# First modulation rounds packed by pairs of feature tiles, and five strips multiplied pair by pair

## The chip, the cores and the metric

The kernel runs on one core of a Trainium2 chip, in one launch. The metric is device time in microseconds (us). Before the change three runs gave 2202.88, 2203.56 and 2204.67 us; the median is 2203.56 us.

## The reference, cut to what matters

Two blocks of two layers each work on 256 tokens with 1024 features, in float32. The change touches only the start of layer 0 of the first block:

```python
mod = jax.nn.silu(c) @ w_ada + b_ada                 # (1, 1024) @ (1024, 3072)
shift, scale, gate = jnp.split(mod, 3, axis=-1)
h = _rmsnorm(x, norm_g) * (1.0 + scale[:, None, :]) + shift[:, None, :]
proj = h @ w_in                                      # (256, 1024) @ (1024, 6680)
(rq, rk, rv, rg, xbc, dt_raw, z, fq, fk, fv, fg, f_raw) = jnp.split(proj, IN_OFFSETS, axis=-1)
...
xbc = jax.nn.silu(_causal_dwconv(xbc, conv_w, conv_b))
dt = jax.nn.softplus(dt_raw + dt_bias)
```

Nothing can be multiplied by w_in before h is there, and a feature tile of h needs the norm of x and that tile's shift and scale, which are columns of w_ada.

## The kernel before, in words

Weights lie in device memory as one stream of *strips* in the order of their use (WPLAN, `wall`), each 128 partitions by up to 1024 columns, 512 KB. `_fetch` (L483) loads a strip into a tile `raw`, and splits it: ScalarE (ACT) copies it, rounded, to `hi` (L476), VectorE (DVE) subtracts that to get `lo` (L503). The tiles `hi` and `lo` have three buffers each; strip 3, one of EXTRA, uses tiles that are free at that time (`ret_o`, `fox_v`). `mm3` (L526) multiplies with three matmuls for each of the eight feature tiles of h (L530 to L532), each 128x256 here, so a strip takes 24. Strips 0 to 3 are B and C of the state-space branch, and each goes through `conv4`, a convolution of four taps in three DVE instructions on the PSUM bank (L472, tile `cv_y`). Strip 4 holds dt and the forget gates and goes into `dtf`, some 25 small DVE instructions. Strips 5 and on alternate between convolutions and parts of the attention branch. PSUM has three banks `mm`, three `aux` and two `tr`.

The modulation is made in *rounds* of 512 columns of w_ada: `ada_load` brings 2 MB in two transfers, `ada_round` (L683) multiplies them by silu(c) on TensorE (PE; L697, 32 records of the trace for each transfer), ACT copies the row, PE transposes it (L704), and DVE adds the bias into `mod`. Rounds 0 and 1 are the shift, rounds 2 and 3 the scale of feature tiles 0 to 3 and 4 to 7. They come in the order 0, 2, 1, 3 (FIRST_ROUNDS), so that `first_norm` can finish h (tiles `h_hi` on ACT, `h_lo` on DVE) for tiles 0 to 3 after two rounds and for tiles 4 to 7 after the other two. Before that x is normalised: squares on ACT, sums on DVE, a column sum on PE (L614), a reciprocal root in some ten small DVE instructions, a broadcast on PE (L623), and eight products into `qk_fox`. `spread` (L749) broadcasts silu(c) over the partitions for later rounds, which DVE does itself (L740). Here the names read `yd`, `qk_ret`, `xs`, `xdt` for the four tiles that hold the two transfers of a round, in turn, since these tiles are free at that time.

All transfers of weights are issued by SyncE (SP) in the order of the program. The order of the instructions on an engine is fixed when the program is built: it follows the order of the code, priorities (`prio`) and `issue_after`, which puts an instruction behind another. On the chip each engine takes its instructions in that order and waits for the one at the head.

Of the kernel before, what the change touches and what calls it, by code (L numbers as in the profile page):

```python
# [10 lines left out]
F32 = mybir.dt.float32  # L11
# [7 lines left out]
P = 128  # L19
# [149 lines left out]

FIRST_ROUNDS = (0, 2, 1, 3)


def _ada_plan():
    s = []
    for name, rounds in (("w_ada", 6), ("ada_w_2", 12)):
        for l in range(2):
            order = FIRST_ROUNDS + (4, 5) if (name, l) == ("w_ada", 0) else range(rounds)
            for r in order:  # L180
                for q in range(4):
                    if (1 if name == "w_ada" else 2, l, r) in ON_PE:
                        s.append((name, l, _full(2, 256 * q), ((512 * r, 512),)))
                    else:
                        s.append((name, l, None, ((512 * r + P * q, P),)))
    return s
# [178 lines left out]
class Kern:  # L365
# [117 lines left out]
    def _fetch(self):  # L483
        spec = WPLAN[self.wpos]
        w = _width(spec)
        nm = f"{self.wpos}"
        raw = self.wp.tile([P, 1024], F32, tag="raw", name="raw" + nm, bufs=RAW_BUFS)
        self.nc.sync.dma_start(out=raw[:, :w], in_=self.wall[self.woff:self.woff + P * w].rearrange("(p w) -> p w", p=P))
        if self.wpos in EXTRA and self.wpos < N_PLAN1:
            hi, lo = [self.bt([P, 1024], tag, FR, 1) for tag in ("ret_o", "fox_v")]  # L490
        elif self.wpos in EXTRA:
            hi, lo = [self.s4([P, 1024], FR, h + nm) for h in ("hi", "lo")]
        else:
            hi = self.wp.tile([P, 1024], FR, tag="hi", name="hi" + nm)
# [71 lines left out]
        while self.bg:  # L566
            self.bg.popleft()()

    def proj_f(self, name, act, T0, T, behind=None):

        w = self.strip(name)
        ps = self.mm_bank()
        with self.tc.issue_after(behind.ins) if behind else nullcontext():
            self.mm3(ps[:, :T], w, [(a[:, T0:T0 + T], b[:, T0:T0 + T]) for a, b in act])
        return ps[:, :T]

    def proj_t(self, name, act, tiles):
# [92 lines left out]
    def ada_load(self, which, l, r, tags=None):  # L670

        parts = []
        m = 2 if tags else 1
        for q in range(0, 4, m):
            spec = APLAN[self.apos]
            assert spec[0] == ("w_ada", "ada_w_2")[which - 1] and spec[1] == l and spec[3][0][0] == 512 * r
            t = self.bt([P, 2, 1024], tags[q // 2], F32, 1) if tags else self.s4([P, 1, 1024], F32, f"ada{which}{l}_{r}")
            n = m * P * 1024
            self.nc.sync.dma_start(out=t, in_=self.aall[self.aoff:self.aoff + n].rearrange("(m p w) -> p m w", p=P, m=m))
            self.aoff += n  # L680
            self.apos += m
            parts += [t[:, i] for i in range(m)]
        return parts  # L683

    def ada_round(self, which, l, r, parts):

        nc = self.nc
        nm = f"ada{which}{l}_{r}"
# [12 lines left out]
        s = self.ncpool.tile([P, P], F32, tag="ada_s", name=nm + "s", bufs=1)  # L701
        self.act(s, ps[:, :P], AF.Copy)
        pt = self.ps("tr")
        nc.tensor.transpose(pt[:, :P], s, self.ident)  # L704
        b = self.v(("b_ada%d" if which == 1 else "ada_b2%d") % l, 4 * r, 4)
        for i, m in enumerate(self.mods[which, l]):
            col = 0 if which == 1 else 1 + i
            self.add(m[:, 4 * r:4 * r + 4], pt[:, col:P:32], b)

    def new_mods(self, which, l):  # L710
        n = 24 if which == 1 else 48
# [34 lines left out]
        if q == 3:  # L746
            self.adaq.popleft()

    def spread(self, which, pool):  # L749

        self.cb[which] = [pool.tile([P, 1024], F32, tag=f"cb{which}{i}", name=f"cb{which}{i}", bufs=1) for i in range(which)]

        def piece(i, half):
            ps = self.ps("aux")
# [90 lines left out]
    def layer1(self, l):  # L845
# [6 lines left out]
        lo = self.bt([P, KD, 256], "h_lo", FR, 1)  # L852
        h = self.pairs(hi, lo, 8)
        if l == 0:
            self.first_norm(rb, h)
        else:
            mod = self.mods[1, l][0]
            self.modulate(self.b1, [([x[:, k] for k in range(KD)], 0, 256, self.v(f"norm_g{l}"), mod[:, 8:16], mod[:, 0:8], rb)], h)
            self.hold(HOLD)
        mod = self.mods[1, l][0]  # L860
        BC = self.bt([P, 4, 256], "BC", F32, 1)
        for n in range(4):

            behind = self.round_mm[(1, 0) + BEHIND[n]] if l == 0 and n < len(BEHIND) else None
            self.conv4(l, self.proj_f("w_in", h, 0, T, behind), 8 + n, BC[:, n])
            self.pump()
        ps = self.proj_f("w_in", h, 0, T)
        self.dtf(l, ps)
        cbm = self.bt([P, 2, 384], "cbm", F32, 1)
        for g in range(2):  # L870
# [108 lines left out]
    def first_norm(self, rb, h):  # L979
# [7 lines left out]
        for half in range(2):
            for r in FIRST_ROUNDS[2 * half:2 * half + 2]:
                self.adaq.popleft()
                if r != FIRST_ROUNDS[0]:  # L990
                    self.ada_round(1, 0, r, self.ada_load(1, 0, r, self.first_tags()))
                if r == FIRST_ROUNDS[SPREAD]:
                    for f in self.spread(1, self.b1):
                        f()
            if half == 0:
                for _ in range(3):
                    self._fetch()
            mod = self.mods[1, 0][0]
            c = slice(4 * half, 4 * half + 4)
            self.stt(a[:, c], mod[:, 8 + 4 * half:12 + 4 * half], 1.0, g[:, c], ALU.add, ALU.mult)  # L1000
            for k in range(4 * half, 4 * half + 4):
# [16 lines left out]
    def dtf(self, l, ps):  # L1018
        nc = self.nc
        sg, cr = self.c("sgn"), self.c("carry")  # L1020
        b = self.ncpool.tile([P, 4], F32, tag="dtf_b", name=f"dtf_b{l}")
        self.mul(b[:, 0:1], self.v(f"dtf_b{l}"), sg)

        self.act(b[:, 1:2], self.v(f"a_log{l}"), AF.Exp)
        self.ts(b[:, 1:2], b[:, 1:2], -1.0, ALU.mult)
# [825 lines left out]
    def run(self):  # L1851
# [102 lines left out]
```

## Time and profile before

| | us |
|---|---|
| median of three runs | 2203.56 |
| profiled execution, its own time | 2205.41 |
| its span, from the first to the last instruction | 2203.6 |
| PE busy | 2150.6 (98%) |
| DVE busy | 1714.0 (78%) |
| ACT busy | 1001.4 (45%) |

The profiled execution is one run, 1.85 us above the median. PE is busy nearly everywhere but at the start and in a few short stretches, so what matters is what PE waits for and when.

### The profile page before, as it was taken

What the parts mean: (1) busy time and instruction counts of PE and PEld (TensorE: products, weight loads), DVE (VectorE), ACT (ScalarE), POOL (GpSimd) and SP (SyncE); (2) the same over time, 40 slices, a digit from 0 to 9 for tenths busy, and PEclk for the clock granted to TensorE, in tenths of its full rate; (3) what the DMA queues carried; (4) which work ended last, traced back from release to release, by engine and by line L of the source; (5) the groups of instructions that cost most, each with busy time, mean ns of one, the idle gap of its engine ahead of it and who ended that gap; (6) DMA issues with size and microseconds to landing.
All of it is one profiled execution on the core that took longest, in us unless ns stands there. A gap on an engine that the chain in (4) does not pass through costs nothing. (4 is left out here: it accounts for less than half of the span.)

```text
span 2203.6 us, 38200 instructions
## 1 busy us (share of the span) xinstructions
PE 2150.6 (98%) x14481; PEld 1918.2 (87%) x14481; DVE 1714.0 (78%) x3551; ACT 1001.4 (45%) x1828; POOL 69.8 (3%) x654
## 2 busy tenths in 40 slices
PE   6999999999999999999999999999999999999999
PEld 5999989898877888888888888888888999999999
DVE  5986889888885899775575777666689977577977
ACT  4556455555445423432333443324355434445654
POOL 0000000000000000000000000000000000000000
PEclk9999999999999999999999999999999999999999
DMA  7665846467321134335353244453432353674665
GB/s 292 197 197 175 270 134 199 146 199 268 105 67 54 54 109 150 97 110 158 123 157 103 88 133 120 131 176 124 131 106 82 115 168 114 213 250 146 189 193 162
DMA packets 98088, 330.71 MB, mean 150 GB/s; under 512 B 10864, under 2 KB 14320, under 8 KB 97648
## 3 DMA queue, kind: packets, MB, share of 16 engines
q1 hardware_dynamic: 97456, 326.47, 46.5%
q8 instruction: 114, 1.87, 0.3%
q0 software_dynamic: 448, 1.81, 0.2%
q14 instruction: 70, 0.57, 0.1%
HBM read 325.08 MB, written 3.15 MB: 149 GB/s over the span
## 5 line engine op out<-in xcount | busy, mean ns | idle before, releaser
L476 ACT ACTIVATE hi<-raw 128x1024 fp32r<-128x1024 f32 (+3 forms) x494 | 492.0, 997 | 712.8 <-PE mm L531 445.0
L503 DVE TENSOR_TENSOR lo<-raw,hi 128x1024 fp32r<-128x1024 f32 (+3 forms) x494 | 564.8, 1144 | 234.9 <-ACT hi L476 231.2
L530 PE MATMUL mm<-h,hi 128*128 128x512 f32 (+1 forms) x1296 | 445.2, 344 | 3.3 <-ACT th L476 1.2
L532 PE MATMUL mm<-h,lo 128*128 128x512 f32 (+1 forms) x1296 | 441.9, 342 | 2.6 <-DVE lo L503 2.6
L531 PE MATMUL mm<-h,hi 128*128 128x512 f32 (+1 forms) x1296 | 441.9, 342 | 0.4 <-DVE h L472 0.4
L530 PEld LDWEIGHTS mm<-h,hi 128*128 128x128 f32 x1296 | 244.7, 189 | 32.8 <-ACT h L476 1.5
L532 PEld LDWEIGHTS mm<-h,lo 128*128 128x128 f32 x1296 | 245.0, 189 | 31.9 <-DVE lo L503 3.4
L531 PEld LDWEIGHTS mm<-h,hi 128*128 128x128 f32 x1296 | 244.8, 189 | 30.0 <-DVE h L472 0.8
L530 PE MATMUL mm<-hi,h 128*128 128x256 f32 x608 | 173.4, 285 | 1.6 <-ACT h L476 1.6
L531 PE MATMUL mm<-lo,h 128*128 128x256 f32 x608 | 172.5, 284 | 1.2 <-DVE lo L503 1.2
L532 PE MATMUL mm<-hi,h 128*128 128x256 f32 x608 | 173.0, 285 | 0.1
L530 PE MATMUL mm<-h_hi,hi 128*128 128x256 f32 x512 | 145.4, 285 | 4.2 <-ACT h_hi L476 2.5
L532 PE MATMUL mm<-h_hi,lo 128*128 128x256 f32 x512 | 145.3, 285 | 1.1 <-DVE lo L503 1.0
L531 PE MATMUL mm<-h_lo,hi 128*128 128x256 f32 x512 | 145.6, 286 | 0.5 <-DVE h_lo L454 0.5
L472 DVE SCALAR_TENSOR_TENSOR cv<-glu,vec,cv 128x512 f32<-128x512 f32 (+1 forms) x240 | 136.3, 613 | 2.5 <-ACT cv L476 2.5
L740 DVE SCALAR_TENSOR_TENSOR ada<-ada,cb 128x1024 f32<-128x1024 f32 x104 | 126.7, 1219 | 1.4 <-DMA ada<-aall 0.9
L530 PEld LDWEIGHTS mm<-hi,h 128*128 128x128 f32 x608 | 115.6, 190 | 3.3 <-ACT h L476 2.4
L531 PEld LDWEIGHTS mm<-lo,h 128*128 128x128 f32 x608 | 115.5, 190 | 2.1 <-DVE lo L503 1.4
L532 PEld LDWEIGHTS mm<-hi,h 128*128 128x128 f32 x608 | 115.7, 190 | 1.0 <-DVE h L472 0.7
L530 PEld LDWEIGHTS mm<-h_hi,hi 128*128 128x128 f32 x512 | 97.8, 191 | 5.3 <-ACT h_hi L476 2.9
L532 PEld LDWEIGHTS mm<-h_hi,lo 128*128 128x128 f32 x512 | 97.9, 192 | 1.7 <-DVE lo L503 1.7
L531 PEld LDWEIGHTS mm<-h_lo,hi 128*128 128x128 f32 x512 | 97.9, 191 | 1.3 <-DVE h_lo L454 0.9
(675 smaller groups left out, 4826.4 us busy)
## 6 DMA issues: line engine op xcount, KB each, us to landing
raw<-wall SPq DMA_DIRECT2D x400, 512.0 KB, 3.7
ada<-aall SPq DMA_DIRECT2D x120, 512.0 KB, 4.1
raw<-wall SPq DMA_DIRECT2D x32, 384.0 KB, 3.1
raw<-wall SPq DMA_DIRECT2D x32, 320.0 KB, 3.0
raw<-wall SPq DMA_DIRECT2D x32, 256.0 KB, 2.6
yd<-aall SPq DMA_DIRECT2D x2, 1024.0 KB, 10.4
qk_ret<-aall SPq DMA_DIRECT2D x2, 1024.0 KB, 11.4
xs<-aall SPq DMA_DIRECT2D x2, 1024.0 KB, 10.6
```

Source lines behind the costliest of these rows:

```text
L472: return self.nc.vector.scalar_tensor_tensor(out=out, in0=a, scalar=s, in1=b, op0=op0, op1=op1)
L476: return self.nc.scalar.activation(out, a, f, bias=bias, scale=scale, **kw)
L503: self.last_lo = self.nc.vector.tensor_tensor(lo[:, :w], raw[:, :w], hi[:, :w].bitcast(F32), op=ALU.subtract)
L530: mm(ps, ah, bh, start=first and n == 0, stop=False)
L531: mm(ps, ah, bl, start=False, stop=False)
L532: self.last_mm = mm(ps, al, bh, start=False, stop=last and n == len(A) - 1)
L740: nc.vector.scalar_tensor_tensor(out=out, in0=raw, scalar=1.0, in1=self.cb[which][i], op0=ALU.mult, op1=ALU.mult, accum_out=m[:, n:n + 1])
```

## The change

The first four rounds of layer 0 are cut in another way: round r now holds 256 columns of shift and 256 of scale, those of feature tiles 2r and 2r+1. Each round then finishes one pair of tiles. The rounds come in the order 0, 1, 2, 3, and x comes ahead of them. Five strips, not three, are fetched ahead, the fifth into more free tiles; two of them are loaded into the buffers of tag `ada`. After round 1 all five strips are multiplied with tiles 0 to 3 (60 matmuls), after round 2 with tiles 4 and 5 (30), after round 3 with tiles 6 and 7 (30), in five PSUM banks that stay open. The text below calls these pass 1, pass 2 and pass 3. `spread` goes behind pass 1. Rotary tables and some small preparations are put behind the split of strip 6, the tables with a lower priority too.

```diff
-EXTRA = (3, 72, 244, 423)
+EXTRA = (3, 4, 72, 244, 423)
...
+FIRST_STRIPS = 5
+ROT_LATE = 260
...
-FIRST_ROUNDS = (0, 2, 1, 3)
+def _mixed(which, l, r):
+    return (which, l) == (1, 0) and r < 4
...
+                        cols = ((256 * r, 256), (1024 + 256 * r, 256)) if _mixed(which, l, r) else ((512 * r, 512),)
+                        s.append((name, l, _full(2, 256 * q), cols))
...
-        raw = self.wp.tile([P, 1024], F32, tag="raw", name="raw" + nm, bufs=RAW_BUFS)
+        early = self.wpos in EXTRA and self.wpos < FIRST_STRIPS
+        tag, bufs = ("ada", 2) if early else ("raw", RAW_BUFS)
+        raw = self.wp.tile([P, 1024], F32, tag=tag, name="raw" + nm, bufs=bufs)
...
+            tags = ("fox_k", "fox_o") if self.wpos == 4 else ("ret_o", "fox_v")
+            hi, lo = [self.bt([P, 1024], tag, FR, 1) for tag in tags]
...
-        for half in range(2):
-            for r in FIRST_ROUNDS[2 * half:2 * half + 2]:
-                self.adaq.popleft()
-                if r != FIRST_ROUNDS[0]:
+        strips, pss = [], []
+        for r in range(4):
+            self.adaq.popleft()
+            if r:
+                with self.tc.issue_after(self.last_mm.ins):
                     self.ada_round(1, 0, r, self.ada_load(1, 0, r, self.first_tags()))
-                if r == FIRST_ROUNDS[SPREAD]:
-                    for f in self.spread(1, self.b1):
-                        f()
-            if half == 0:
-                for _ in range(3):
+            if r == 1:
+                for _ in range(FIRST_STRIPS):
                     self._fetch()
+                for n in range(FIRST_STRIPS):
+                    strips.append(self.strip("w_in", 0))
+                    pss.append(self.ps("mm" if n < 3 else "aux")[:, :256])
...
+            if r:
+
+                ks = slice(0 if r == 1 else 2 * r, 2 * r + 2)
+                behind = self.last_ada
+                for w, ps in zip(strips, pss):
+                    with self.tc.issue_after(behind.ins):
+                        self.mm3(ps, w[ks], h[ks], first=r == 1, last=r == 3)
+                    behind = self.last_mm
+            if r == 1:
+                with self.tc.issue_after(self.last_mm.ins):
+                    for f in self.spread(1, self.b1, "tr"):
+                        f()
+        for _ in range(2):
+            self._fetch()
         self.load_group(self.b1, 1, "cst")
...
+        self.start_ends = self.last_hi.ins, self.last_lo.ins
...
+        with self.behind_start(), self.prio(ROT_LATE):
+            self.rotary_tables()
+        return pss
```

The first order is PE's at the start of the program, before the change: `ones,acc` is the column sum of the norm, `cst,rs13y` the broadcast of its root, `cst,cT` is `spread`, and the tiles `yd`, `qk_ret`, `xs`, `xdt` are transfers of the rounds.

```order
L697 MATMUL tr_98<-yd_93,cT 32x128 x16
L697 MATMUL tr_98<-qk_ret_95,cT 32x128 x16
L704 MATMUL tr_133<-cst_69,ada_0s 128x128
L697 MATMUL tr_213<-xs_209,cT 32x128
L614 MATMUL aux_162<-ones,acc_139 128x1 x2
L697 MATMUL tr_213<-xs_209,cT 32x128 x15
L623 MATMUL aux_181<-cst_69,rs13y 128x128 x2
L757 MATMUL aux_197<-cst_69,cT 128x128 x4
```

The same place after the change.

```order
L702 MATMUL tr_101<-yd_96,cT 32x128
L619 MATMUL aux_162<-ones,acc_139 128x1 x2
L702 MATMUL tr_101<-yd_96,cT 32x128 x15
L628 MATMUL aux_181<-cst_69,rs13y 128x128 x2
L702 MATMUL tr_101<-qk_ret_98,cT 32x128 x16
L709 MATMUL tr_136<-cst_69,ada_0s 128x128
L702 MATMUL tr_207<-xs_203,cT 32x128 x16
L702 MATMUL tr_207<-xdt_205,cT 32x128 x16
```

The second half of round 0 has moved behind the broadcast of the norm, and round 1 (`xs`, `xdt`) behind both.

The second place is PE where the rounds of the second half of h stand. Before, the last round (round 3: `xs`, `xdt`) stands between strip 0 (`mm_409`) and strip 1 (`mm_448`).

```order
L530 MATMUL mm_409<-h_hi_184,hi_253 128x256
L531 MATMUL mm_409<-h_lo_185,hi_253 128x256
L532 MATMUL mm_409<-h_hi_184,lo_254 128x256
L697 MATMUL tr_328<-xs_324,cT 32x128 x16
L697 MATMUL tr_328<-xdt_326,cT 32x128 x16
L530 MATMUL mm_448<-h_hi_184,hi_259 128x256
```

After, `aux_279` is strip 4 at the end of pass 1, and `mm_275` strip 0 at the start of pass 2.

```order
L537 MATMUL aux_279<-h_lo_185,fox_k_271 128x256
L538 MATMUL aux_279<-h_hi_184,fox_o_272 128x256
L766 MATMUL tr_348<-cst_69,cT 128x128 x4
L766 MATMUL tr_354<-cst_69,cT 128x128 x4
L702 MATMUL tr_364<-yd_360,cT 32x128 x16
L702 MATMUL tr_364<-qk_ret_362,cT 32x128 x16
L709 MATMUL tr_399<-cst_69,ada_2s 128x128
L536 MATMUL mm_275<-h_hi_184,hi_247 128x256
```

Round 2 stands behind the whole of pass 1 and `spread`, and pass 2 behind round 2; round 3 stands likewise behind pass 2, and pass 3 behind round 3.

The third place is DVE around the first `h_lo`. Before, after the eight products of the norm come the splits of strips 0 to 2 (L503) and then the tiles of h.

```order
L503 TENSOR_TENSOR lo_254<-raw_251,hi_253 128x1024
L454 TENSOR_TENSOR mod_97<-tr_248,vec_67 128x4
L503 TENSOR_TENSOR lo_260<-raw_257,hi_259 128x1024
L503 TENSOR_TENSOR lo_266<-raw_263,hi_265 128x1024
L472 SCALAR_TENSOR_TENSOR modA_first<-mod_97,vec_137 128x4
L469 TENSOR_SCALAR qk_fox_186<-qk_fox_186,modA_first,mod_97 128x256
L454 TENSOR_TENSOR h_lo_185<-qk_fox_186,h_hi_184 128x256
```

After, from round 1's bias to the last tile of h of pass 1; L509 is the split, `lo_248` strip 0's.

```order
L457 TENSOR_TENSOR mod_100<-tr_242,vec_67 128x2x2
L475 SCALAR_TENSOR_TENSOR modA_first<-mod_100,vec_94 128x2
L509 TENSOR_TENSOR lo_248<-raw_245,hi_247 128x1024
L472 TENSOR_SCALAR qk_fox_186<-qk_fox_186,modA_first,mod_100 128x256 x2
L457 TENSOR_TENSOR h_lo_185<-qk_fox_186,h_hi_184 128x256
L509 TENSOR_TENSOR lo_254<-raw_251,hi_253 128x1024
L509 TENSOR_TENSOR lo_260<-raw_257,hi_259 128x1024
L457 TENSOR_TENSOR h_lo_185<-qk_fox_186,h_hi_184 128x256
```

Three splits now stand between round 1's bias and the last `h_lo` that pass 1 needs.

## Rows read from the trace of the kernel before

**Rows 1.** The page, first part: busy us, share of the span, instructions.

```profile
PE 2150.6 (98%) x14481; PEld 1918.2 (87%) x14481; DVE 1714.0 (78%) x3551; ACT 1001.4 (45%) x1828; POOL 69.8 (3%) x654
```

**Rows 2.** Busy time of the engines in stretches of the first 80 us.

```profile
core 0: us, PE busy (x) PEld busy (x) DVE busy (x) ACT busy (x) POOL busy (x), PEclk, DMA share, GB/s
0.00:20.00 20.00, 7.82 (x101) 5.52 (x101) 6.01 (x27) 5.30 (x13) 0.20 (x4) 1.00 0.90 348
20.00:40.00 20.00, 17.23 (x216) 14.89 (x216) 11.08 (x32) 8.33 (x16) 0.00 (x0) 0.91 0.94 364
30.00:35.00 5.00, 3.80 (x29) 2.83 (x33) 2.98 (x9) 2.15 (x5) 0.00 (x0) 0.80 0.98 385
35.00:40.00 5.00, 5.00 (x78) 4.59 (x70) 1.34 (x8) 1.79 (x5) 0.00 (x0) 0.86 0.75 303
40.00:60.00 20.00, 17.90 (x142) 17.19 (x141) 18.74 (x45) 14.74 (x25) 1.95 (x2) 1.00 0.45 140
60.00:80.00 20.00, 19.23 (x158) 18.68 (x157) 19.87 (x45) 12.16 (x21) 0.00 (x0) 1.00 0.55 162
```

**Rows 3.** Timeline, 7 to 38 us: start, busy us, engine, line, operation, [idle before, releaser].

```profile
7.59 1.93 PE L697 MATMUL tr<-yd,cT 128*32 128x128 f32 x32 [7.59 <-DMA yd<-aall]
...
12.59 0.42 ACT L476 ACTIVATE acc<-x 128x256 f32<-128x256 f32 x1 [0.26 <-DMA x<-xT]
...
20.38 1.22 PE L623 MATMUL aux<-cst,rs13y 128*128 128x128 f32 x4 [0.56 <-DVE rs13y L472]
...
21.39 3.62 PE L757 MATMUL aux<-cst,cT 128*128 128x128 f32 x16
...
27.26 1.08 PE L697 MATMUL tr<-yd,cT 128*32 128x128 f32 x32
...
34.31 1.94 PE L697 MATMUL tr<-xs,cT 128*32 128x128 f32 x32
...
36.02 1.25 PE L697 MATMUL tr<-xdt,cT 128*32 128x128 f32 x32
```

**Rows 4.** The last transfer of the rounds: its issue, then its us to landing.

```profile
26.67 0.37 SPq L679 DMA_DIRECT2D xdt<-aall  x1
...
xdt<-aall SPq DMA_DIRECT2D x1, 1024.0 KB, 6.0
```

**Rows 5.** Instructions in order of time, 38 to 43 us: second half of h.

```profile
38.09 0.16 DVE L454 TENSOR_TENSOR mod<-tr,vec 128x4 f32<-128x4 f32 x1 [4.50 <-PE tr L704]
...
39.13 0.41 DVE L469 TENSOR_SCALAR qk_fox<-qk_fox,modA_first,mod 128x256 f32<-128x256 f32 x1 [0.53 <-ACT h_hi L476]
...
39.58 0.42 DVE L454 TENSOR_TENSOR h_lo<-qk_fox,h_hi 128x256 fp32r<-128x256 f32 x1
...
41.73 0.42 DVE L454 TENSOR_TENSOR h_lo<-qk_fox,h_hi 128x256 fp32r<-128x256 f32 x1
```

**Rows 6.** DVE and PE in order of time, 45 to 65 us: strips 3 to 8.

```profile
45.45 0.28 DVE L472 SCALAR_TENSOR_TENSOR rot_r<-rot_n,rot_r 128x128 f32<-128x128 f32 x1
45.65 0.47 DVE L472 SCALAR_TENSOR_TENSOR cv_y<-mm,vec,cv_y 128x255 f32<-128x255 f32 x1
45.67 0.36 PE L530 MATMUL mm<-h_hi,ret_o 128*128 128x256 f32 x1 [0.58 <-ACT hi L476]
...
48.59 0.28 PE L530 MATMUL mm<-h_hi,hi 128*128 128x256 f32 x1
...
50.90 0.43 DVE L472 SCALAR_TENSOR_TENSOR BC<-cv_t,cv_y 128x256 f32<-128x256 f32 x1 [1.11 <-ACT cv_t L476]
...
53.39 0.35 PE L530 MATMUL mm<-h_hi,hi 128*128 128x256 f32 x1 [1.41 <-DVE cv_y L472]
...
63.48 1.22 DVE L503 TENSOR_TENSOR lo<-raw,hi 128x1024 fp32r<-128x1024 f32 x1
64.61 0.42 DVE L472 SCALAR_TENSOR_TENSOR sp<-sp,sp 128x256 f32<-128x256 f32 x1
64.75 0.39 PE L532 MATMUL mm<-h_hi,lo 128*128 128x256 f32 x1 [0.73 <-DVE lo L503]
```

More of the change, by code (lines that the diff above doesn't have):

```diff
@@ L178, in _ada_plan @@
         for l in range(2):
-            order = FIRST_ROUNDS + (4, 5) if (name, l) == ("w_ada", 0) else range(rounds)
-            for r in order:
+            which = 1 if name == "w_ada" else 2
+            for r in range(rounds):
                 for q in range(4):
-                    if (1 if name == "w_ada" else 2, l, r) in ON_PE:
-                        s.append((name, l, _full(2, 256 * q), ((512 * r, 512),)))
+                    if (which, l, r) in ON_PE:
+                        cols = ((256 * r, 256), (1024 + 256 * r, 256)) if _mixed(which, l, r) else ((512 * r, 512),)
+                        s.append((name, l, _full(2, 256 * q), cols))
                     else:
@@ L567, in drain, with proj_f @@
             self.bg.popleft()()
-    def proj_f(self, name, act, T0, T, behind=None):
+    def proj_f(self, name, act, T0, T):
         w = self.strip(name)
         ps = self.mm_bank()
-        with self.tc.issue_after(behind.ins) if behind else nullcontext():
-            self.mm3(ps[:, :T], w, [(a[:, T0:T0 + T], b[:, T0:T0 + T]) for a, b in act])
+        self.mm3(ps[:, :T], w, [(a[:, T0:T0 + T], b[:, T0:T0 + T]) for a, b in act])
         return ps[:, :T]
@@ L675, in ada_load @@
             spec = APLAN[self.apos]
-            assert spec[0] == ("w_ada", "ada_w_2")[which - 1] and spec[1] == l and spec[3][0][0] == 512 * r
+            assert spec[0] == ("w_ada", "ada_w_2")[which - 1] and spec[1] == l and spec[3][0][0] == (256 if _mixed(which, l, r) else 512) * r
             t = self.bt([P, 2, 1024], tags[q // 2], F32, 1) if tags else self.s4([P, 1, 1024], F32, f"ada{which}{l}_{r}")
@@ L707, in ada_round @@
             col = 0 if which == 1 else 1 + i
-            self.add(m[:, 4 * r:4 * r + 4], pt[:, col:P:32], b)
+            if _mixed(which, l, r):
+                two = lambda a: a[:, 0:16].rearrange("p (a k) -> p a k", a=2)[:, :, 2 * r:2 * r + 2]
+                self.add(two(m), pt[:, 0:P:32].rearrange("p (a k) -> p a k", a=2), two(self.v("b_ada0")))
+            else:
+                self.add(m[:, 4 * r:4 * r + 4], pt[:, col:P:32], b)
     def new_mods(self, which, l):
@@ L747, in ada_step, with spread @@
             self.adaq.popleft()
-    def spread(self, which, pool):
+    def spread(self, which, pool, tag="aux"):
         self.cb[which] = [pool.tile([P, 1024], F32, tag=f"cb{which}{i}", name=f"cb{which}{i}", bufs=1) for i in range(which)]
         def piece(i, half):
-            ps = self.ps("aux")
+            ps = self.ps(tag)
             for k in range(4):
@@ L854, in layer1 @@
         if l == 0:
-            self.first_norm(rb, h)
+            first = self.first_norm(rb, h)
         else:
+            first = []
             mod = self.mods[1, l][0]
@@ L862, in layer1 @@
         for n in range(4):
-            behind = self.round_mm[(1, 0) + BEHIND[n]] if l == 0 and n < len(BEHIND) else None
-            self.conv4(l, self.proj_f("w_in", h, 0, T, behind), 8 + n, BC[:, n])
+            self.conv4(l, first.pop(0) if first else self.proj_f("w_in", h, 0, T), 8 + n, BC[:, n])
             self.pump()
-        ps = self.proj_f("w_in", h, 0, T)
+        ps = first.pop(0) if first else self.proj_f("w_in", h, 0, T)
         self.dtf(l, ps)
@@ L986, in first_norm @@
         g = self.v("norm_g0")
[L987 to L996 removed]
+        strips, pss = [], []
[3 more added lines that the diff above has]
+                with self.tc.issue_after(self.last_mm.ins):
+                    self.ada_round(1, 0, r, self.ada_load(1, 0, r, self.first_tags()))
+            if r == 1:
+                for _ in range(FIRST_STRIPS):
                     self._fetch()
+                for n in range(FIRST_STRIPS):
+                    strips.append(self.strip("w_in", 0))
+                    pss.append(self.ps("mm" if n < 3 else "aux")[:, :256])
             mod = self.mods[1, 0][0]
[L999 to L1001 removed]
+            c = slice(2 * r, 2 * r + 2)
+            self.stt(a[:, c], mod[:, 8 + 2 * r:10 + 2 * r], 1.0, g[:, c], ALU.add, ALU.mult)
+            for k in range(2 * r, 2 * r + 2):
                 ak, sh = a[:, k:k + 1], mod[:, k:k + 1]
@@ L1009, in first_norm, with behind_start @@
         self.act(self.idr, self.ident, AF.Copy)
-        self.act(self.fmask, self.c("foxmask"), AF.Copy)
-        self.rotary_tables()
+        with self.behind_start():
+            self.act(self.fmask, self.c("foxmask"), AF.Copy)
+        with self.behind_start(), self.prio(ROT_LATE):
+            self.rotary_tables()
+        return pss
+    @contextmanager
+    def behind_start(self):
+        with self.tc.issue_after(self.start_ends[0]), self.tc.issue_after(self.start_ends[1]):
+            yield
     def first_tags(self):
@@ L1021, in dtf @@
         b = self.ncpool.tile([P, 4], F32, tag="dtf_b", name=f"dtf_b{l}")
-        self.mul(b[:, 0:1], self.v(f"dtf_b{l}"), sg)
-        self.act(b[:, 1:2], self.v(f"a_log{l}"), AF.Exp)
-        self.ts(b[:, 1:2], b[:, 1:2], -1.0, ALU.mult)
+        with self.behind_start():
+            self.mul(b[:, 0:1], self.v(f"dtf_b{l}"), sg)
+            self.act(b[:, 1:2], self.v(f"a_log{l}"), AF.Exp)
+            self.ts(b[:, 1:2], b[:, 1:2], -1.0, ALU.mult)
         z = self.bt([P, 256], "dtf_z", bufs=1)
```

7 lines of the change are left out of this document (2 added, 5 removed).

## The prediction

> **What bounds the kernel now.** The page's first part comes first: PE is busy 98% of the span, 53.0 us short of it, and DVE 78% [rows 1]. The table of stretches tells where PE is not busy: 12.2 us short in the first 20 us, 2.8 in the next 20, 2.1 from 40 to 60, 0.8 from 60 to 80, 17.8 of the 53.0 in all [rows 2]. In the same table DVE fills up: 11.1 of 20 us from 20 to 40, 18.7 from 40 to 60, 19.9 from 60 to 80. So the start has two limits one after the other: until about 42 us PE and DVE wait for rounds and for h, and from then on DVE has more to do than PE can wait for. The timeline shows the join. The last `h_lo` ends at 42.15 (41.73 + 0.42) [rows 5]; strip 5 starts at 53.39 after 1.41 us of idle PE, and strip 8 waits for its split on DVE, which ends at 64.70, and goes on at 64.75 [rows 6]. From there PE is full. So a change at the start is worth what it moves that point, if what follows keeps pace.
>
> **The change part by part.** The computation stays the same, 120 strip matmuls for five strips and four rounds. What is changed is the order in which PE takes them, so I follow PE's new order with the old durations.
>
> *x first.* Now x is the first megabyte. The first megabyte was there at 7.59, x at 12.59, and from there to the end of the broadcast of the norm were 9.0 us (20.38 + 1.22 - 12.59) [rows 3]. That puts the broadcast's end at 16.6 instead of 21.6.
>
> *Rounds 0 and 1.* The second half of round 0 is now behind the broadcast on PE. Its 32 records took 1.93 us at the start, 1.08 at 27.26, and 1.94 at 34.31, where the granted clock falls [rows 2, 3]. In a start with gaps I take 1.93: 18.5. From the end of a round's matmuls (36.02 + 1.25 = 37.27) to the bias on DVE are 0.8 us [rows 3, 5], in which PE transposes, so round 1 runs from 19.3 to 23.2. Its bytes are there by then: four megabytes behind x at 364 GB/s, 11.5 us, 19.1 [rows 2]. Its bias is added at 24.0.
>
> *The last h_lo of pass 1.* On DVE three splits now stand between this bias and the fourth `h_lo`. A split takes 1.13 us to the next start (63.48 to 64.61) [rows 6], an instruction of h 0.4 [rows 5]: 0.4 for the factor and the wait for ACT, 3 x 1.13, and 4 x 0.4 give 29.4. PE can have done only 10 of the 60 matmuls of pass 1 by then.
>
> *Pass 1, spread, round 2.* A strip's 24 matmuls take 2.92 us (45.67 to 48.59), 0.122 each [rows 6]: 50 take 6.1. The clock costs more. Before, the granted clock is 0.80 from 30 to 35 and 0.86 from 35 to 40, together 3.4 us at 1.2 GHz, after PE had issued little while it waited for h [rows 2]. From 23 to 29 it now waits in the same way, so I add half of 3.4: pass 1 ends at 37.2. `spread` took 3.62 [rows 3]; I take half, since it follows 50 matmuls without a gap (bounds 1.8 and 3.6): 39.0. Round 2 takes 2 x 1.08: 41.2. Its bytes don't matter: even round 3's last transfer, which landed at 32.7 (26.67 + 6.0) [rows 4], comes only 2.9 us later for the two strips (1.05 MB) put ahead of it.
>
> *Two chains in a row.* From the end of a round's matmuls to the second DVE instruction on h are 1.9 us (37.27 to 39.13), and four of these at 0.42 follow: 3.5 us [rows 3, 5]. PE has four matmuls to do meanwhile. So the last `h_lo` of pass 2 is there at 44.7, and 26 matmuls later it is 47.9. Round 3 is behind that: 50.1, its chain 53.6, pass 3 56.8. Before, five strips were done at 51.98 (53.39 - 1.41), and h at 42.15. The old order had one chain for four tiles; the new has two, each behind a pass.
>
> *What DVE has then.* Three buffers `hi` belong to strips 0 to 2, which now stay in use until pass 3. So ACT's copy of strip 5 waits for the sixth matmul of pass 3, and its split starts some 1.4 us after the last `h_lo` (0.3 for these and 1.1 for the copy, taken as long as a split): 55.0. From the last `h_lo` to the end of strip 8's split DVE took 22.55 us (42.15 to 64.70). Of that three things go: the rotary tables (12 instructions at 0.20, as from 45.45 to 45.65, 2.4 us), the splits of strips 3 and 4 (2.3), and 1.1 of idle time [rows 6]. This leaves 16.8. Strip 8's split then ends at 71.8, against 64.70: 7.1 us late. PE can't hide it, since strip 5 needs the bank of strip 0, which is free only after its convolution.
>
> *After that.* The rotary tables now come between the splits of strips 12 and 16. Beside a full PE, 2.4 us of DVE cost between nothing and all of it; I take 0.4, since DVE's share falls a little below full from there. PE was full from 64.75 on, so nothing gives back the 7.1 us. The sum is +7.5: 2205.41 + 7.5 = 2212.9 for an execution like the profiled one, which is 1.85 above the median, and 2203.56 + 7.5 = 2211.1, or 2211, for the median.
>
> **The rivals.** *Full clock at the start.* If PE has the higher clock from round 0's second half on, it takes 1.08 instead of 1.93 (0.85), round 1 gains 1.7, and pass 1 its 1.7: 4.2 us less, 2206.9. For it: PE now works in closer sequence there. Against it: 1.93 at 7.59 and 1.94 at 34.31, both after waits [rows 3].
>
> *Half clock in passes 2 and 3.* Each comes after a chain in which PE does nearly nothing for some 3 us, like the wait after which the granted clock fell to 0.80 [rows 2]. At half rate 26 matmuls cost 3.2 us more, two passes 6.4: 2217.5. Against it: the rounds just before keep PE at work. The Trainium skill, page "TensorE: Matmul & The Clock Gate", section "Loop structure matters more than you think", says that a loop nest decides whether matmuls stay at the higher clock, and that waits between bursts lose it. By this rule the three passes would run at the lower clock and the time would be this rival's. The row from 30 to 35 agrees, the 1.00 from 40 to 60, with waits of 1.41 and 0.58 us in it, does not.
>
> *Faster: h is ready earlier.* DVE after the last `h_lo` has 5.8 us less to do than before, net of the wait for strip 5's copy 4.4. So the change wins if the last `h_lo` comes before 46.5 (64.70 - 16.8 - 1.4), us for us. Round 3's bytes allow it: landing at 35.6, 1.1 for its second half, 3.5 of chain, 40.2, which is 6.3 us ahead: 2197.3. Against it stands PE's order, which puts pass 1, `spread`, round 2 and pass 2 before round 3, 20.7 us from 29.4 to 50.1.
>
> *Order of the rest.* The fixed order differs in details down to the last instruction. Some 35 us of PE's waits lie behind 80 us [rows 1, 2]; one tenth of them, 3.5 us, can go either way. It belongs to the range and not to a case.
>
> **How the numbers follow.** About 0.2% (4.4 us) is what a measurement of this kernel tells from no change. Forecast, 55%: 2211, slower, its own terms 2208.0 to 2215. Half clock in the passes, 15%: slower. Full clock, or a saving of like size elsewhere, 22%: within 0.2%. Faster, 8%. So faster 0.08, same 0.22, slower 0.70. The range reaches from 2203.5 (full clock with 3.5 us of luck in the rest) to 2218 (the half-clock case).
>
> **What would show it.** Right: the last `h_lo` near 53.6 and two idle gaps of 2 to 3 us on PE between passes; strip 5 starting near 59; the third matmul of strip 8 waiting for its split near 72; the same lag at 300 us and at the end. Wrong: a last `h_lo` before 46.5, round 3's matmuls near their landing, strip 8 without a wait, or a lag that shrinks between 100 and 500 us.

## The result, and the profile after

The changed kernel takes 2216.65 us (median of four runs, 2215.20 to 2217.28) against 2203.70 us in the same four rounds. The ratio is 1.0059, with a 95% interval from 1.0047 to 1.0071: 13.0 us slower. The forecast was 2211, slower, with a range from 2203.5 to 2218. The sign, the range and the places are right. The amount, 7.5 us, is 5.5 short of 13.0, and terms that I had priced wrongly cancel each other on the way.

The profiled execution took 2215.20 us with a span of 2213.4, 9.8 us more than that of before. The page's first part shows the work unchanged [rows 1]:

```profile
PE 2155.4 (97%) x14481; PEld 1921.3 (87%) x14481; DVE 1714.6 (77%) x3553; ACT 1001.7 (45%) x1828; POOL 69.7 (3%) x654
```

The busy time in stretches of the kernel after (columns as in [rows 2]: busy us with the number of records for each engine, then the granted clock of PE, the share of the DMA engines and GB/s):

```profile
0.00:20.00 20.00, 8.37 (x105) 6.29 (x109) 9.07 (x36) 5.24 (x13) 0.20 (x4) 1.00 0.90 347
25.00:30.00 5.00, 3.02 (x15) 2.81 (x15) 4.62 (x5) 2.44 (x3) 0.00 (x0) 0.67 1.03 409
30.00:35.00 5.00, 5.00 (x31) 5.00 (x31) 0.00 (x0) 0.00 (x0) 0.00 (x0) 0.65 1.02 408
...
40.00:60.00 20.00, 14.28 (x126) 12.49 (x126) 8.27 (x20) 7.00 (x13) 1.90 (x2) 0.83 0.21 68
60.00:80.00 20.00, 17.50 (x136) 16.68 (x137) 19.85 (x48) 11.66 (x22) 0.00 (x0) 1.00 0.33 101
...
26.90:33.70 6.80, 6.29 (x30) 6.30 (x31) 2.72 (x4) 0.54 (x1) 0.00 (x0) 0.51 1.03 408
44.00:47.40 3.40, 3.40 (x18) 3.40 (x18) 0.00 (x0) 0.00 (x0) 0.00 (x0) 0.53 0.00 0
54.20:57.60 3.40, 3.40 (x18) 3.40 (x18) 2.05 (x2) 2.96 (x5) 1.58 (x2) 0.53 0.00 0
```

From 40 to 60 us, where DVE was full before (18.74 of 20), it is now busy for 8.27, and from 60 to 80 it is full again. That is the predicted shape: DVE stands idle while PE goes through pass and round in turn, and then becomes the limit. What I had not put into the sum is the clock. The last three rows each lie in one of the three passes: PE runs at half clock (1.2 GHz) for 6.8, 3.4 and 3.4 us, 13.6 in all, where the same column of before shows 3.4 in the first 80 us [rows 2]. The first 20 us (26 of before) stand outside this count: the trace holds no clock record there, and the column shows 1.00 all the same (last section). One stretch in pass 1 was in the sum; those in passes 2 and 3 were a rival.

PE in order of time (columns as in [rows 3]; `tr` rows of 32 records are the transfers of a round, the row of L766 is `spread`):

```profile
18.60 1.67 PE L702 MATMUL tr<-xs,cT 128*32 128x128 f32 x32
20.09 1.05 PE L702 MATMUL tr<-xdt,cT 128*32 128x128 f32 x32
...
27.41 0.58 PE L537 MATMUL mm<-h_lo,hi 128*128 128x256 f32 x1 [1.99 <-DVE h_lo L457]
27.79 0.41 PE L538 MATMUL mm<-h_hi,lo 128*128 128x256 f32 x1
28.00 0.41 PE L536 MATMUL mm<-h_hi,hi 128*128 128x256 f32 x1
...
36.17 1.95 PE L766 MATMUL tr<-cst,cT 128*128 128x128 f32 x16
38.04 1.08 PE L702 MATMUL tr<-yd,cT 128*32 128x128 f32 x32
...
41.87 0.38 PE L536 MATMUL mm<-h_hi,hi 128*128 128x256 f32 x1 [1.08 <-ACT h_hi L479]
...
43.56 0.43 PE L537 MATMUL mm<-h_lo,hi 128*128 128x256 f32 x1 [0.17 <-DVE h_lo L457]
...
48.36 1.08 PE L702 MATMUL tr<-xs,cT 128*32 128x128 f32 x32
49.26 1.06 PE L702 MATMUL tr<-xdt,cT 128*32 128x128 f32 x32
...
53.88 0.50 PE L537 MATMUL mm<-h_lo,hi 128*128 128x256 f32 x1 [0.17 <-DVE h_lo L457]
...
60.10 0.36 PE L536 MATMUL mm<-h_hi,hi 128*128 128x256 f32 x1 [1.36 <-DVE cv_y L475]
...
73.02 0.39 PE L538 MATMUL mm<-h_hi,lo 128*128 128x256 f32 x1 [0.97 <-DVE lo L509]
```

The order is the one that the prediction walked through: pass 1 (from 27.41), `spread`, round 2, a chain, pass 2, round 3, a chain, pass 3. At half clock a strip matmul starts 0.21 us after the one before (27.79, 28.00), where it was 0.122 [rows 6]. Strip 5 starts at 60.10 instead of 53.39, strip 8's third matmul at 73.02 instead of 64.75.

DVE in order of time (the number in brackets is its idle time ahead of the row):

```profile
40.82 0.16 DVE L457 TENSOR_TENSOR mod<-tr,vec 128x4 f32<-128x4 f32 x1 [11.20 <-PE tr L709]
...
43.08 0.42 DVE L457 TENSOR_TENSOR h_lo<-qk_fox,h_hi 128x256 fp32r<-128x256 f32 x1
51.14 0.16 DVE L457 TENSOR_TENSOR mod<-tr,vec 128x4 f32<-128x4 f32 x1 [7.63 <-PE tr L709]
...
53.40 0.42 DVE L457 TENSOR_TENSOR h_lo<-qk_fox,h_hi 128x256 fp32r<-128x256 f32 x1
55.50 2.50 DVE L509 TENSOR_TENSOR lo<-raw,hi 128x1024 fp32r<-128x1024 f32 x2 [1.68 <-ACT hi L479]
...
71.75 1.22 DVE L509 TENSOR_TENSOR lo<-raw,hi 128x1024 fp32r<-128x1024 f32 x1
```

DVE waits 11.2 and 7.6 us for PE, then 1.68 for strip 5's copy. The last `h_lo` ends at 53.82 (before 42.15), strip 8's split at 72.97 (before 64.70).

How the loss runs on from there I read by setting the start of each strip's split on DVE against that of before; strips count from 0, and the 40th split is that of strip 40. The lag is 8.3 us at strip 8 (63.5 us of before), 10.7 at the 40th split (196 us), 10.6 at the 120th (487 us), and 9.7 at the 490th (2187 us).

### The profile page after: what moved, and what is told of

It reads as the page before. It is cut to its first block, busy times and chain, and to the rows that moved or that the text cites. A ratio compares the mean times of both kernels' runs of the same rounds, so it can differ in the third digit from the quotient of the medians.

```text
span 2213.4 us, 38206 instructions
## 1 busy us (share of the span) xinstructions
PE 2155.4 (97%) x14481; PEld 1921.3 (87%) x14481; DVE 1714.6 (77%) x3553; ACT 1001.7 (45%) x1828; POOL 69.7 (3%) x654
## 5 line engine op out<-in xcount | busy, mean ns | idle before, releaser
L509 DVE TENSOR_TENSOR lo<-raw,hi 128x1024 fp32r<-128x1024 f32 (+3 forms) x493 | 563.9, 1144 | 237.2 <-ACT hi L479 233.9
```

## The experiments

My theory: the loss comes from PE's order, in which each of rounds 2 and 3 stands behind a pass and each pass behind a chain from the round to h, and half clock in the passes makes it longer. Rivals: the clock alone, the buffers that strips 0 to 2 hold, the number of strips, the packing and the order of the loads, the rotary tables. The table puts the runs together (medians against before in the same rounds; the columns in the middle are from each run's profiled execution).

| run | last `h_lo` ends | strip 5 starts on PE | strip 8's split ends | lag at 40th / 120th split | median, us (against before) |
|---|---|---|---|---|---|
| before | 42.15 | 53.39 | 64.70 | | |
| after | 53.82 | 60.10 | 72.97 | +10.7 / +10.6 | 2216.65 (+13.0) |
| e9, after again | 53.81 | 60.17 | 73.03 | +11.8 / +12.1 | 2215.52 (+12.4) |
| e1, PE kept at work | 49.98 | 56.01 | 70.15 | +9.2 / +9.7 | 2212.86 (+9.3) |
| e3, three strips | 47.05 | 60.46 | 70.15 | +8.9 / +8.8 | 2213.21 (+9.7) |
| e7, tables among convolutions | 51.41 | 57.54 | 68.05 | +9.0 / +9.4 | 2216.95 (+13.9) |
| e2, rounds first | 43.10 | 49.67 | 62.54 | +2.4 / +2.9 | 2205.93 (+2.4) |
| e5, whole strips | 40.25 | 52.73 | 61.59 | -0.2 / +0.1 | 2205.14 (+1.6) |
| e8, rounds first, 36 extra | 41.81 | 48.38 | 61.24 | 0.0 / +0.2 | 2203.47 (+0.4) |
| e6, e8 and tables | 41.96 | 48.28 | 58.78 | +0.8 / +1.9 | 2203.22 (+0.1) |
| e10, h first | 41.63 | 48.90 | 56.58 | -1.2 / -0.5 | 2205.04 (+1.9) |

### e5: the packing without the products by pairs

```diff
-            if r:
-
-                ks = slice(0 if r == 1 else 2 * r, 2 * r + 2)
+            if r == 1:
+                with self.tc.issue_after(self.last_ada.ins):
+                    for f in self.spread(1, self.b1, "tr"):
+                        f()
+            if r == 3:
                 behind = self.last_ada
                 for w, ps in zip(strips, pss):
                     with self.tc.issue_after(behind.ins):
-                        self.mm3(ps, w[ks], h[ks], first=r == 1, last=r == 3)
+                        self.mm3(ps, w, h)
                     behind = self.last_mm
-            if r == 1:
-                with self.tc.issue_after(self.last_mm.ins):
-                    for f in self.spread(1, self.b1, "tr"):
-                        f()
```

> One part alone: x first and the rounds repacked by pairs of tiles as in the changed kernel, but no products by tile pairs: rounds 1, 2 and 3 come as their bytes do, and the five strips run whole behind the last one, as in the kernel before (spread behind round 1). Theory: the last h_lo follows round 3's last bytes, which landed at 35.7 in the changed kernel, by 1.1 to 1.9 us of matmuls and 3.5 us of chain, 40.3 to 41.2, earlier than 42.15 in the kernel before; strip 8's split ends at 60 to 64, time 2197 to 2204, so the whole loss lies in the passes between the rounds. Rival (the repacking or the order of loads itself costs time, or the order of the rest of the program does): strip 8's split over 68 or, with it earlier than 65, a time over 2209 all the same.

Measured: ratio 1.0011 [1.0002, 1.0020], 2205.14 us. PE of this kernel:

```profile
33.35 1.68 PE L702 MATMUL tr<-xs,cT 128*32 128x128 f32 x32
35.66 1.08 PE L702 MATMUL tr<-xdt,cT 128*32 128x128 f32 x32 [0.63 <-DMA xdt<-aall]
36.67 0.38 PE L536 MATMUL mm<-h_hi,hi 128*128 128x256 f32 x1
...
52.73 0.36 PE L536 MATMUL mm<-h_hi,hi 128*128 128x256 f32 x1
```

Round 3 follows its bytes, the last `h_lo` ends at 40.25 and strip 8's split at 61.59, as expected. So 11.5 of the 13.0 us are in the passes between the rounds (2216.65 - 2205.14); packing, loads and the rest of the program leave 1.6. The time missed its bound of 2204 by 1.1 us. One part of it can be read: h is there 1.9 us earlier than before, but all five strips' matmuls now lie behind round 3, so strip 5 starts only 0.7 us earlier. And the 3.1 us by which strip 8's split is early are gone by the 40th split (-0.2 in the table).

### e2: the same passes, with the rounds ahead of them

```diff
-        for r in range(4):
-            self.adaq.popleft()
-            if r:
-                with self.tc.issue_after(self.last_mm.ins):
-                    self.ada_round(1, 0, r, self.ada_load(1, 0, r, self.first_tags()))
...
-                for w, ps in zip(strips, pss):
-                    with self.tc.issue_after(behind.ins):
-                        self.mm3(ps, w[ks], h[ks], first=r == 1, last=r == 3)
...
+        b = round_(1, self.last_mm)
...
+        tiles(1)
+        b = part(1, range(2), b)
+        b = round_(2, b)
+        tiles(2)
+        b = part(1, range(2, 5), b)
+        b = round_(3, b)
+        tiles(3)
+        b = part(2, range(5), b)
+        b = part(3, range(5), b)
```

Here `round_` makes a round, `tiles` its pair of tiles of h, and `part` multiplies the strips named with the tiles of a pass; `spread` follows pass 3.

> The changed kernel with the rounds put ahead of the passes on PE: strips 0 and 1 of pass 1, round 2, strips 2 to 4 of pass 1, round 3, then passes 2 and 3, and the transposes of spread last. Same loads, same packing by tile pairs. Theory (PE's order pass, round, pass, round makes the lag, since each chain of 3.5 us stands behind a pass): round 3's matmuls run near 38 to 40 instead of 48.4 to 50.3, last h_lo 42 to 45 instead of 53.8, strip 8's split ends at 61 to 65 (64.7 in the kernel before), time 2198 to 2205. Rival (the lag comes from the three buffers that strips 0 to 2 hold until pass 3, or from what DVE has to do after h, whatever the order of the rounds): strip 8's split ends later than 69, time over 2210.

Measured: ratio 1.0013 [1.0004, 1.0022], 2205.93 us. PE of this kernel:

```profile
37.64 1.08 PE L702 MATMUL tr<-xs,cT 128*32 128x128 f32 x32
38.53 1.06 PE L702 MATMUL tr<-xdt,cT 128*32 128x128 f32 x32
...
49.67 0.35 PE L536 MATMUL mm<-h_hi,hi 128*128 128x256 f32 x1 [0.80 <-DVE cv_y L475]
...
62.59 0.39 PE L538 MATMUL mm<-h_hi,lo 128*128 128x256 f32 x1 [0.96 <-DVE lo L509]
```

Same bytes, same packing, the same 120 matmuls, the same three buffers held until pass 3: the change of order on PE alone gives back 10.7 of 13.0 us. This settles the cause, as the order with what it does to the clock: the two later stretches of half clock are gone too, and `spread` (1.95 us) no longer stands before round 2. The buffers are not it, since DVE still waits for strip 5's copy, 2.11 us here and 1.68 in the changed kernel:

```profile
45.21 1.23 DVE L509 TENSOR_TENSOR lo<-raw,hi 128x1024 fp32r<-128x1024 f32 x1 [2.11 <-ACT hi L479]
```

### e1: PE kept at work in the chains

```diff
-        nc.tensor.transpose(pt[:, :P], s, self.ident)
+        self.last_tr = nc.tensor.transpose(pt[:, :P], s, self.ident)
...
-                behind = self.last_ada
+                behind = self.warm(self.last_tr, h[0][0], 36 if r == 1 else 18)
```

> The changed kernel with PE kept at work in the three chains: after the transpose of rounds 1, 2 and 3 PE gets 36, 18 and 18 extra matmuls whose result nobody reads (about 4.5 and 2 x 2.2 us at full rate), ahead of each pass. Theory (two chains in a row on PE, and on top of them half clock in the passes, which cost 3.3 + 1.65 + 1.65 us of the 8.3 by which strip 8's split is late): the granted clock stays up, matmuls of the passes start 0.12 us apart instead of 0.213, the last h_lo comes at 48.5 to 50 instead of 53.8, strip 8's split ends near 67 to 68.5, time 2210 to 2212. Rival (the chain from round to h and DVE's splits set the pace alone, the clock is hidden beside DVE): last h_lo within 1 us of 53.8, time within 2 us of the changed kernel's 2216.7.

Measured: ratio 1.0046 [1.0033, 1.0058], 2212.86 us. Stretches and PE of this kernel:

```profile
20.00:30.00 10.00, 9.50 (x114) 9.03 (x107) 9.14 (x17) 7.21 (x10) 0.00 (x0) 1.00 1.03 408
30.00:40.00 10.00, 9.54 (x130) 9.15 (x129) 0.81 (x4) 2.57 (x5) 0.00 (x0) 1.00 1.03 407
40.00:60.00 20.00, 16.63 (x172) 15.65 (x172) 11.38 (x27) 7.81 (x16) 1.90 (x2) 0.94 0.31 101
60.00:80.00 20.00, 17.85 (x126) 17.12 (x125) 17.64 (x41) 10.66 (x19) 0.00 (x0) 0.89 0.25 77
```

```profile
21.93 4.55 PE L563 MATMUL tr<-h_hi 128*128 128x256 f32 x36
26.32 0.28 PE L536 MATMUL mm<-h_hi,hi 128*128 128x256 f32 x1
...
56.01 0.35 PE L536 MATMUL mm<-h_hi,hi 128*128 128x256 f32 x1 [2.60 <-DVE cv_y L475]
```

The clock stays at 1.00 through pass 1 (the extra matmuls lie in the wait for DVE), and the last `h_lo` comes 3.8 us earlier. The median falls by 3.8 us to 2212.86, just beyond the expected bound; strip 8's split comes 2.8 us earlier, less than expected. The intervals of the two ratios overlap (1.0033 to 1.0058 here, 1.0047 to 1.0071 for the changed kernel), and against e9 the median falls by 2.7. So the clock costs some 2 to 4 of the 13.0. Part came back: PE now waits 2.60 us for a convolution at strip 5, and the clock falls in other places between 50 and 80 us.

### e3: three strips by pairs

```diff
-EXTRA = (3, 4, 72, 244, 423)
+EXTRA = (3, 72, 244, 423)
-FIRST_STRIPS = 5
+FIRST_STRIPS = 3
```

> The changed kernel with three strips instead of five advanced by tile pairs; strips 3 and 4 come whole behind them. Passes have 36, 18 and 18 matmuls instead of 60, 30 and 30. Theory: the 24 and 12 matmuls that no longer stand ahead of rounds 2 and 3 (0.213 us each at half rate, 5.1 and at most 2.6 us) go from the way to the last h_lo, which comes at 47 to 50; but strips 3 and 4 now need buffers that strips 0 and 1 hold until pass 3, and their two splits (2.3 us) move behind the last h_lo, so strip 8's split ends at 69 to 71.5, time 2209 to 2213. Rival (the number of strips doesn't matter, only that there are two chains in a row): last h_lo over 52, time 2216 or more.

Measured: ratio 1.0050 [1.0037, 1.0062], 2213.21 us, 0.2 above the bound; last `h_lo` 47.05, strip 8's split 70.15, both as expected. 6.8 us earlier with h, and only 2.8 at strip 8. The theory's reason holds for a part of this only: strip 3 still has tiles of its own and is split at 39.59, ahead of the last `h_lo`, so one split (strip 4's, 1.1 us) has moved behind it and not two. The other 2.8 us are waits of DVE: 1.57, 2.52 and 0.39 us in this kernel against 1.68 in the changed one, while PE, at half clock from 47.8 to 58.0 us, ends pass 3 and does strip 3 whole and then strip 4. The longest of them is for a convolution:

```profile
48.61 1.23 DVE L509 TENSOR_TENSOR lo<-raw,hi 128x1024 fp32r<-128x1024 f32 x1 [1.57 <-PE mm L538]
58.03 2.04 DVE L475 SCALAR_TENSOR_TENSOR cv_y<-mm,vec,cv_y 128x255 f32<-128x255 f32 x5 [2.52 <-ACT cv_y L479]
68.93 1.22 DVE L509 TENSOR_TENSOR lo<-raw,hi 128x1024 fp32r<-128x1024 f32 x1
```

### e7 and e9: the tables, and the changed kernel once more

```diff
-        with self.behind_start(), self.prio(ROT_LATE):
+        with self.behind_start():
             self.rotary_tables()
```

> The changed kernel with the rotary tables back near the start: their twelve DVE instructions stand behind the splits of strips 5 and 6, among the first convolutions, instead of between the splits of strips 12 and 16. Theory (DVE's backlog between the last h_lo and strip 8's split sets where PE can go on, and what stands later there is nearly free): strip 8's split ends 2 to 2.4 us later than 72.97, the lag at 90 to 200 us grows by as much, less the 0.4 at most that the tables cost at their late place, time 2217.5 to 2219. Rival (the tables' late place is what costs the 2 us by which the lag grows between 73 and 196 us): strip 8's split later, but the lag at 200 us as in the changed kernel or less, time 2215 to 2217.

Measured: ratio 1.0060 [1.0048, 1.0072], 2216.95 us, within the rival's bounds: no difference that can be told from the changed kernel. The theory's lag at strip 8 failed. With the tables early, most of DVE's work on dt (tile `sp`) stands behind strip 8's split and not ahead of it, as in e6 and e10 too (strip 8's column of the table doesn't compare these three with the others), so this run doesn't tell what the tables alone cost. In its profiled execution pass 2 ran at full clock, and the last `h_lo` came 2.4 us earlier than in the two executions of the changed kernel: whether the clock falls there is not the same in each execution.

> The changed kernel once more, unchanged, to see which part of its loss repeats: the medians differ by 13.0 us, the two profiled executions by 9.8. Theory (nearly all of it is made by 80 us, and the rest is in stretches of half clock later in the program that come and go from one execution to the next): the same last h_lo, strip 5 and strip 8 within 0.3 us, the same steps of the lag at 190 to 210 us, and a difference at the end of 9 to 14 us that changes only where the granted clock falls. Rival (there is a fixed further loss in the rest that the first profile missed): the lag at 2187 us over 12 with no difference in the clock.

Measured: ratio 1.0054 [1.0042, 1.0066], 2215.52 us. The first 73 us repeat within 0.1 us. At the 120th split the lag is 12.1 instead of 10.6, after a clock of 0.91 from 60 to 80 us. Between the 140th and the 150th split (551 and 628 us) the lag falls by 1.5 us in one and 3.1 in the other, and there it is the kernel before that has more of half clock; at 1695 us it is the changed kernel. Before, then after (stretches as above):

```profile
550.00:570.00 20.00, 18.01 (x157) 16.84 (x148) 14.96 (x64) 7.19 (x17) 3.53 (x32) 0.83 0.27 85
...
1695.00:1705.00 10.00, 10.00 (x77) 9.45 (x76) 9.90 (x21) 7.13 (x14) 0.43 (x5) 1.00 0.11 28
```

```profile
550.00:570.00 20.00, 18.22 (x183) 17.22 (x182) 17.96 (x47) 11.72 (x23) 3.58 (x31) 0.91 0.62 188
1695.00:1705.00 10.00, 7.98 (x39) 4.69 (x37) 7.18 (x14) 3.09 (x7) 0.63 (x7) 0.83 0.06 25
```

So the profiled pair shows 9.8 us where the medians show 13.0: after's profiled execution is 1.4 us below its median, before's 1.7 above its own. By 490 us the lag is 10.6 to 12.1, and the interval of the ratio is 10.4 to 15.6 us, so the rest up to 13.0 needs no cause of its own. That such stretches move the time from one execution to the next is borne out by the 59 executions of the kernel before that were timed beside the experiments: the 10 with a mean granted clock of 0.998 took 2201.0 us on average, the 13 with 0.994 took 2204.1. That they make the rest of the 13.0 is not shown.

### e8, e6 and e10: towards a faster version

e8 is e2 with the extra matmuls ahead of pass 1, e6 is e8 with the edit of e7:

```diff
         tiles(1)
+        b = self.warm(self.last_tr, h[0][0], 36)
         b = part(1, range(2), b)
```

e10 is e8 with 24 for 36 and with the fourth `h_lo` and the tables earlier on DVE:

```diff
-        tiles(1)
+        with self.prio(-500):
+            tiles(1)
...
-        with self.behind_start(), self.prio(ROT_LATE):
+        with self.tc.issue_after(self.h_end.ins), self.prio(-500):
             self.rotary_tables()
```

> The kernel with the rounds put ahead of the passes, with 36 extra matmuls behind the transpose of round 1, so that strips 0 and 1 of pass 1 run at full clock. Theory: the two strips' 24 matmuls end 2 us or more earlier, round 2 follows its last bytes (30.6) and round 3 its own (35.7), last h_lo at 40.3 to 41.5 instead of 43.1, strip 8's split at 60 to 61.5 instead of 62.4; DVE's backlog is then the only limit and the time gains as much, 2203 to 2205 (2205.9 without). Rival (PE's half clock there was hidden behind the landing of the rounds): last h_lo within 0.5 us of 43.1 and the time as without.

Measured: ratio 1.0003 [0.9994, 1.0012], 2203.47 us; last `h_lo` 41.81, strip 8's split 61.24. Against before in the same rounds that is 0.4 us, where e2 has 2.4, so the extra matmuls may be worth 2.0 us, but the intervals overlap (1.0004 to 1.0012). The traces don't bear the 2.0 out either: e8 is 1.3 us ahead of e2 at strip 8, but only 0.2 at the 30th split (134 us of before), and the 2.4 us between them at the 40th are a wait of PE for ACT's `ret_fox`, 2.15 us at 165.5 us, that e2 has and e8 has not. The time is that of before.

> The rounds ahead of the passes, the 36 extra matmuls ahead of pass 1, and the rotary tables among the first convolutions. Meant as a version that might beat both kernels. Theory (what DVE has to do before strip 8's split is the limit): the tables put 2 to 2.4 us in front of strip 8's split, so it is no better than the same kernel with the tables late, 2204 to 2207. Rival (the tables' late place costs more, since PE waits for DVE at 142 and 163 us in the kernel with the rounds first): 2200 to 2203, below the kernel before.

Measured: ratio 1.0002 [0.9994, 1.0011], 2203.22 us, between the two expectations and equal to e8 and to before.

> The rounds ahead of the passes, as before, with three small moves that the earlier runs point to: the fourth h_lo on DVE ahead of the splits of strips 1 to 4 (it stood behind two of them and came at 27.5), so that 24 extra matmuls do instead of 36; the rotary tables behind the last h_lo, where DVE waited 2.11 us for strip 5's copy. Theory (PE is held by the rounds' bytes up to the last h_lo and by DVE's backlog from there to strip 8's split): last h_lo at 40.3 to 41.8, the tables hidden in the wait, strip 8's split at 60 to 61.5 and nothing of the tables left for later, so 0.5 to 2 us less than the 2203.5 of the kernel with 36 extra matmuls: 2201.5 to 2203, at or just below the kernel before. Rival (what is gained before 70 us is lost again to the order of the rest by 200 us, as in the runs before): 2203 to 2205.

Measured: ratio 1.0006 [0.9997, 1.0015], 2205.04 us: the expected gain didn't come, and no version beats the kernel before. DVE in e10 (then stretches of after, e8 and e10, each from 80 to 200 us):

```profile
24.90 0.76 DVE L1010 TENSOR_TENSOR h_lo<-qk_fox,h_hi 128x256 fp32r<-128x256 f32 x2
...
41.20 0.43 DVE L1010 TENSOR_TENSOR h_lo<-qk_fox,h_hi 128x256 fp32r<-128x256 f32 x1
```

```profile
80.00:200.00 120.00, 117.43 (x932) 107.46 (x933) 99.12 (x227) 72.64 (x158) 0.00 (x0) 1.00 0.60 185
```

```profile
80.00:200.00 120.00, 117.66 (x930) 107.35 (x929) 95.55 (x217) 73.08 (x168) 0.00 (x0) 1.00 0.58 183
```

```profile
80.00:200.00 120.00, 118.80 (x946) 109.06 (x945) 95.35 (x216) 70.86 (x167) 0.00 (x0) 1.00 0.58 185
```

The kernel before has 118.82 busy there, e10 118.80. In e10 the lag stays between -1.2 and -1.3 from the 10th to the 40th split; in e8 it goes from -3.5 at strip 8 to 0.0, in e2 from -2.2 to +2.4, in the changed kernel from +8.3 to +10.7. So a part of each loss is not in the start at all: in another order of the rest PE waits 1.2 to 1.4 us longer between 80 and 200 us, and 3.7 in e2 (115.12 busy). The largest such wait in the changed kernel is 1.08 us for ACT's `hi` at 152 us; e7 and e6, which have the tables early, have it too (1.15 and 1.08 us), so the tables' late place is not what makes it. And e10, which has none of this, is no faster: in its profiled execution the lag grows from -1.2 at the 40th split to +1.5 at the 490th, 1.5 of it beside a stretch of half clock at 1689 us that before does not have. Why its median is 1.9 above before's stays open.

## Why the prediction was right, and where its sizes were wrong

*The mechanism: right, and shown.* Rounds 2 and 3 behind the passes make the last `h_lo` late and leave DVE idle; the order on PE alone (e2) gives back 10.7 of 13.0 us.

*x first, rounds 0 and 1: right in kind, 2 us too dear.* Round 1 began at 18.60 instead of 19.3, and I took the low rate for all of it: its second transfer took 1.05 us instead of 1.93. So the rival of full clock at the start came about in part. The fourth `h_lo` ended at 27.35 instead of 29.4.

*Pass 1: half clock for longer.* I added 1.7 us. The clock was 0.51 from 26.9 to 33.7, twice the 3.4 us of before, and from the fourth `h_lo` to `spread` it took 8.8 us instead of 7.8.

*`spread`, round 2, the chains: right.* 1.95 for half of 3.62; 3.5 us from the end of a round's matmuls to the second `h_lo` (40.0 to 43.50, 50.32 to 53.82) as in the sum.

*Passes 2 and 3: the step that failed.* I put the half clock there at 15%, on the ground that "the rounds just before keep PE at work". They did not: both passes show 0.53 for 3.4 us. Pass 2 took 4.9 us (43.50 to 48.36) instead of 3.2. In the Trainium skill, page "TensorE: Matmul & The Clock Gate", section "Loop structure matters more than you think", waits between bursts cost matmuls the higher clock; the trace agrees, with 0.53 in both passes after chains of 3.5 us in which PE had five instructions, though in e7's execution pass 2 kept 1.00. The rival priced this at 2217.5, 0.9 from the median. But it reached that with 3.2 us a pass, where a pass lost 1.7, and e1, which takes away the fall in pass 1 too, is worth 3.8 at most. So its closeness to the median is luck and no proof of its size.

*The last `h_lo`: 53.6 forecast, 53.82 measured, by cancellation.* The 2.05 us of the earlier start were taken back by pass 1 (+1.0) and pass 2 (+1.7), less some 0.2 us in each of rounds 2 and 3, which took 1.96 instead of 2.16. That the two numbers agree is luck.

*DVE's backlog: near.* The copy of strip 5 waited for its buffer as said (split at 55.50, forecast 55.0), and from there to strip 8's split DVE took 17.5 us instead of 16.8. The lag at strip 8 is 8.3, forecast 7.1.

*After that: the other mis-sized term.* I gave the rest 0.4 us for the tables and set the order of the rest aside as 3.5 us either way. It went the wrong way by 2.4 by 196 us: 0.4 is a wait of PE for a split at 79.88 us that before does not have, 1.4 are waits of PE from 80 to 200. The remaining 0.6, and which place in the order makes these waits, stay open.

*The sum.* 7.5 forecast; +1.2 to strip 8 and +2.0 to the 40th split make 10.7. The last 2.3 to 13.0 lie within the interval of the ratio (10.4 to 15.6 us).

*The rival by which the change wins if the last `h_lo` comes before 46.5, us for us: false as a rule.* e2, e5, e6, e8 and e10 had h there at 40.25 to 43.10, and none is faster than before. Strip 8's split comes earlier by 2.2 to 3.5 us in e2, e5 and e8, but what is gained there is gone by 196 us.

## What to carry to other kernels

When work is moved forward into a wait, look at what it is put in front of: here the products filled PE's wait, but the next link of the chain (round, h) stood behind them in the same queue. Put the chain's links ahead of the fill. And price a short burst after a wait at both clocks; the gain at one place of the trace counts only when the lag is followed to where the order of the program is the same again.

## What the runs showed of the hardware that was not expected

The clock column reads 1.00 where the trace holds no clock record, so a 1.00 in the first microseconds is no evidence for the full rate; the duration of a known operation is. In the changed kernel the first record, at the full clock, begins at 19.86 us, in the kernel before at 26.18. The same 32 records of a round took 1.67 us from 18.60 and 1.05 from 20.09 after, 1.66 from 24.94 and 1.08 from 27.26 before, all in stretches that the column shows as 1.00. The changed kernel thus left the low rate some 6 us earlier.

And 36 matmuls without a use (4.55 us), put into a wait of PE, kept the clock at 1.00 from 20 to 40 us (e1 and e8), where the changed kernel has 0.83. In e10 24 of them did, and its clock stayed at 1.00 up to 500 us; in e1 it fell again from 40 us on (0.94 and 0.89). What they are worth in time is 2 to 4 us in e1; in e8 no gain is shown.
